# A hybrid decoder layer: the first gate/up products directly behind the last output projection, weight sums formed in place, and another layout of the PSUM banks

## The chip, the cores and the metric

The kernel runs on one core of one Trainium2 chip. The metric is the device time of one execution in microseconds; lower is better. Three runs of the kernel before gave 1325.13 to 1326.1 us, with a median of 1325.38 us.

## The reference

One decoder layer over 1024 tokens of width 1024, in float32:

```python
y = jnp.concatenate([fox_out, gla_out], axis=-1) @ w_o          # two kinds of attention
x = layer_norm(DEEPNORM_ALPHA * x + (1.0 + gate_m) * y, ln1_g, ln1_b)
u2 = x * (1.0 + scale_f) + shift_f
h = jax.nn.silu(u2 @ w_gate) * (u2 @ w_up)                      # w_gate, w_up: 1024 x 2816
y2 = h @ w_down
x = layer_norm(DEEPNORM_ALPHA * x + (1.0 + gate_f) * y2, ln2_g, ln2_b)
```

Everything ahead of `y` (the input projection, forgetting attention, gated linear attention) is the same in both kernels.

## The kernel before

**Split numbers.** Each float32 operand of a matmul is split into a high part (`hi`, rounded to the type that TensorE takes at full rate) and the rest (`lo`). `split` (L86 to L88) is one cast on ScalarE and one subtraction on VectorE. A product is the sum of three matmuls: hi x hi, hi x lo, lo x hi.

**The end of the mixer.** The output projection of the forgetting-attention half runs in units of 128 tokens x 512 columns (`mixer_units`, L830): 12 matmuls into the PSUM tile `yo`, then `yp` on VectorE (L848), a multiplication by the gate row `gm` on GpSimd (L849), the residual `r` on VectorE (L850), layer-norm statistics, and the normalisation of `r` on ScalarE (L857). `r` goes to DRAM as `z_d` (L858). There are two halves of 512 tokens with 8 units each. The `w_o` blocks for them are loaded through `load_split` into the weight pools `raw`, `hi` and `lo`, which have three buffers each; `gm` lies in a `raw` buffer until the last unit has used it.

**The feed-forward products.** Gate and up are formed together, 128 columns of each at a time ("block" `f`, 22 of them), with a Strassen-like scheme of 7 products in place of 8: the tokens are cut into two halves of 512, the input width into two halves of 512. Each product is 12 matmuls (`product`, L962): four chunks of 128 of the inner width, three matmuls each. The stationary operands are the weights `B11`, `B21` (the gate block itself), `T1` to `T4` (sums and differences of gate and up) and `B22` (half of up). The moving operands are the transposed tokens: `A11`, `A12` from the first half (`first_operands`, tiles `a1h`, `a1l`), and `A22`, `S1` to `S4` from both halves (`second_operands`, tiles `a`, `s31h`, `s31l`, `s24h`, `s24l`). `second_operands` needs the `r` of the second half, transposes it on TensorE (`u2p`, L873), evacuates it on ScalarE (L874), and forms sums and splits on VectorE and ScalarE.

**A block's products.** `load_block` fetches gate and up into two `raw` buffers. `first_weights` splits the gate block, `sum_weights` forms `t12`, `t34` in slots 4 and 5 and splits them and half of up. The products write PSUM as follows: `p12_a` (A11 x B11) and `p12_b` (A12 x B21) into the first bank of the two-bank tile `c11` (`gu` in the profile), `p6` (S2 x T2) into its second bank, `p7` (S3 x T3) and then A22 x T4 into `x_` (`gx`), `p5` (S1 x T1) and then S4 x B22 into `y_` (`gy`). ScalarE copies the sum of `p12_a` to `u` (L984) before `p12_b` adds to it; VectorE adds the second bank of `c11` to `u` (L992, `hf`). All eight banks are in use: `w0`, `w1` of two banks and `b0` to `b3`, so that two neighbouring blocks have places of their own.

**What sets the order.** The program is traced in the order of the source, which also gives the priorities; a planner then places the instructions of each engine by their readiness in its own cost estimate, gives out the buffers of the pools, and adds the waits. So TensorE's queue mixes matmuls of several products, and each engine's queue is fixed when the program runs. All loads and stores are issued by SyncE (SP) in one queue. `tc.issue_after(ins)` places what is traced under it behind `ins` in the queue of the same engine, without a wait for its end.

**Around the change.** After the last step of attention the code calls `mixer_loads(1)`, `first_operands(xa)`, the eight units of the second half, `second_operands(xb)`, the weights of blocks 0 and 1, `p12_a` and `p12_b` of both, and then the loop over the 22 blocks (L1158 to L1191). The `pt` tiles of attention lie in slots 24 and 25, the `yp` tiles of the first half in slots 4 to 7.

## Time and profile before

| | |
|---|---|
| median of 3 runs | 1325.38 us (1325.13 to 1326.1) |
| profiled execution, whole time | 1324.17 us |
| its span in the profile | 1322.5 us |
| TensorE busy | 1266.0 us (96%) |
| VectorE busy | 762.9 us (58%) |
| ScalarE busy | 487.2 us (37%) |
| granted TensorE clock, mean | 0.988 of full speed |

The busy times are those of one profiled execution, from the first to the last instruction. Matmuls overlap in the pipeline, so a busy TensorE is not one at its peak: a matmul of 512 columns shows some 390 ns, and the next one can start 0.23 us after it. Where the profile names a releaser, it is the instruction whose signal came last.

### The profile page before, as it was taken

What the parts mean: (1) busy time and instruction counts of PE and PEld (TensorE: products, weight loads), DVE (VectorE), ACT (ScalarE), POOL (GpSimd) and SP (SyncE); (2) the same over time, 40 slices, a digit from 0 to 9 for tenths busy, and PEclk for the clock granted to TensorE, in tenths of its full rate; (3) what the DMA queues carried; (4) which work ended last, traced back from release to release, by engine and by line L of the source; (5) the groups of instructions that cost most, each with busy time, mean ns of one, the idle gap of its engine ahead of it and who ended that gap; (6) DMA issues with size and microseconds to landing.
All of it is one profiled execution on the core that took longest, in us unless ns stands there. A gap on an engine that the chain in (4) does not pass through costs nothing.

```text
span 1322.5 us, 16317 instructions
## 1 busy us (share of the span) xinstructions
PE 1266.0 (96%) x6341; PEld 1017.0 (77%) x6341; DVE 762.9 (58%) x1093; ACT 487.2 (37%) x812; POOL 249.9 (19%) x244
## 2 busy tenths in 40 slices
PE   6999999999999999995999999999999999999997
PEld 4888987899876766673887777777777778778885
DVE  7665547732344536668865555565564497484346
ACT  3422255523266567465422232232232232411331
POOL 3400023320133435432000000000000087010004
PEclk9999999999999999996999999999999999999999
DMA  9865611101013207522432222222223384643431
GB/s 297 255 226 176 206 49 32 33 16 58 9 41 98 68 24 223 189 81 95 117 122 80 80 89 72 80 72 88 80 64 96 98 300 159 203 163 126 130 126 64
DMA packets 120414, 151.60 MB, mean 115 GB/s; under 512 B 6432, under 2 KB 83338, under 8 KB 120336
## 3 DMA queue, kind: packets, MB, share of 16 engines
q1 hardware_dynamic: 120336, 150.55, 35.5%
q8 instruction: 50, 0.82, 0.3%
q14 instruction: 28, 0.23, 0.1%
HBM read 122.07 MB, written 24.13 MB: 111 GB/s over the span
## 4 chain that ended last, share of the span: by engine, by line
PE 67%; issue 12%; DMA 7%; DVE 7%; ACT 3%; POOL 2%; SPq 1%; POOLq 0%; DVEq 0%; ACTq 0%
PE gu L967 11%; PE gy L967 6%; PE gx L967 6%; PE dn L1063 5%; PE dn L1064 5%; PE dn L1065 5%; PE pv L756 4%; DMA wc<-in_w_c_dram 4%; PE tr L746 3%; PE acc L330 2%; PE acc L331 2%; PE acc L332 2%; PE acc L100 2%; PE acc L101 2%; PE acc L99 2%
## 5 line engine op out<-in xcount | busy, mean ns | idle before, releaser
L87 ACT CAST hi<-raw 128x1024 fp32r<-128x1024 f32 (+1 forms) x86 | 90.0, 1049 | 289.0 <-PE gy L967 151.7
L88 DVE TENSOR_TENSOR lo<-raw,hi 128x1024 fp32r<-128x1024 f32 (+1 forms) x86 | 122.3, 1424 | 107.6 <-ACT hi L87 107.4
L1036 POOL TENSOR_TENSOR r<-r,l1g 128x1024 f32<-128x1024 f32 x8 | 26.6, 3361 | 453.8 <-DMA l1g<-in_ln_g_dram 453.8
L330 PE MATMUL acc<-hi,uh 128*128 128x264 f32 (+1 forms) x384 | 108.1, 282 | 2.1 <-ACT gr L410 1.3
L332 PE MATMUL acc<-hi,ul 128*128 128x264 f32 (+1 forms) x384 | 108.2, 282 | 0.0
L331 PE MATMUL acc<-lo,uh 128*128 128x264 f32 (+1 forms) x384 | 108.2, 282 | 0.0
L1064 PE MATMUL dn<-lo,hh 128*128 128x512 f32 x256 | 100.5, 392 | 0.0
L1065 PE MATMUL dn<-hi,hl 128*128 128x512 f32 x256 | 100.2, 392 | 0.0
L1063 PE MATMUL dn<-hi,hh 128*128 128x512 f32 x256 | 93.8, 393 | 1.4 <-ACT hi L87 1.4
L992 DVE TENSOR_TENSOR hf<-gu,hf 128x512 f32<-128x512 f32 x22 | 15.2, 691 | 133.3 <-issue 124.0
L721 DVE CUSTOM_DVE_ANT_0 pr<-sc,smask 128x128 f32<-128x128 f32 (+7 forms) x64 | 47.9, 755 | 55.3 <-PE sc L717 31.8
L967 PE MATMUL gu<-a1h,hi 128*128 128x512 f32 x168 | 69.6, 414 | 9.7 <-DVE hf L992 7.1
L87 ACT CAST hi<-t 128x1024 fp32r<-128x1024 f32 x44 | 46.1, 1050 | 85.6 <-PE gu L967 43.8
L330 PEld LDWEIGHTS acc<-hi,uh 128*128 128x128 f32 x384 | 72.2, 188 | 3.2 <-ACT gr L410 1.5
L331 PEld LDWEIGHTS acc<-lo,uh 128*128 128x128 f32 x384 | 72.2, 188 | 0.7 <-issue 0.3
L332 PEld LDWEIGHTS acc<-hi,ul 128*128 128x128 f32 x384 | 72.1, 188 | 0.3 <-issue 0.2
L88 DVE TENSOR_TENSOR lo<-t,hi 128x1024 fp32r<-128x1024 f32 x44 | 53.8, 1225 | 30.2 <-ACT hi L87 29.8
L967 PE MATMUL gu<-a1h,lo 128*128 128x512 f32 x168 | 67.7, 403 | 2.9 <-DVE lo L88 2.9
L967 PE MATMUL gu<-a1l,hi 128*128 128x512 f32 x168 | 67.4, 401 | 0.0
L731 POOL TENSOR_SCALAR pr<-pr,sm 128x128 f32<-128x128 f32 (+7 forms) x64 | 52.0, 816 | 57.5 <-DVE sm L728 57.1
L756 PE MATMUL pv<-pt,fv 128*64 128x256 f32 x320 | 61.5, 396 | 0.5 <-DVE ofl L88 0.5
L751 ACT COPY pt<-tr 128x512 f32<-128x512 f32 x80 | 46.1, 582 | 41.0 <-PE tr L746 39.2
(298 smaller groups left out, 3183.0 us busy)
## 6 DMA issues: line engine op xcount, KB each, us to landing
raw<-in_w_down_dram SPq DMA_DIRECT2D x44, 512.0 KB, 4.9
wc<-in_w_c_dram SPq DMA_DIRECT2D x32, 512.0 KB, 4.3
raw<-in_w_gate_dram SPq DMA_DIRECT2D x22, 512.0 KB, 3.9
raw<-in_w_up_dram SPq DMA_DIRECT2D x22, 512.0 KB, 4.0
h_d<-hf SPq DMA_DIRECT2D x22, 512.0 KB, 4.1
hr<-h_d SPq DMA_DIRECT2D x22, 512.0 KB, 3.8
wc<-in_w_c_dram SPq DMA_DIRECT2D x32, 256.0 KB, 6.6
raw<-in_w_in_dram SPq DMA_DIRECT2D x15, 512.0 KB, 3.9
```

Of the source, the lines that this page charges most:

```text
L87: nc.scalar.copy(dst_hi, src)
L88: nc.vector.tensor_tensor(dst_lo, src, dst_hi.bitcast(F32), op=ALU.subtract)
L330: nc.tensor.matmul(ps, uh[k][:, ts], wh[:, k % 4, :], start=k == 0, stop=False)
L331: nc.tensor.matmul(ps, uh[k][:, ts], wl[:, k % 4, :], start=False, stop=False)
L332: nc.tensor.matmul(ps, ul[k][:, ts], wh[:, k % 4, :], start=False, stop=k == NK - 1)
L721: nc.vector.tensor_tensor_reduce(t[:, 0:nk], sc[:, 0:nk], smask[:, S - nk : S], op0=ALU.add, op1=ALU.min, scale=-1.0, scalar=3e38, accum_o ...
L731: nc.gpsimd.tensor_scalar(t[:, 0:nk], t[:, 0:nk], sm[:, 2:3], 1.0, op0=ALU.mult, op1=ALU.mult)
L756: nc.tensor.matmul(pv[64 * par : 64 * par + 64, 0:256], fv_t(kb)[:, 64 * h : 64 * h + 64], pt[:, par, a * 256 : (a + 1) * 256], start=kb == 0,
L967: nc.tensor.matmul(ps, x, y, start=start and j == 0 and i == 0, stop=j == NJ - 1 and i == 2, skip_group_check=not start,)
L1063: nc.tensor.matmul(ps, hh, wh, start=i == 0 and a == 0, stop=False)
L1064: nc.tensor.matmul(ps, hh, wl, start=False, stop=False)
L1065: nc.tensor.matmul(ps, hl, wh, start=False, stop=i == NF // 2 - 1 and a == 1)
```

## The change

The last `yo` matmul is remembered in `last["yo"]`. The gate blocks 0, 1 and 2 are loaded and split early: blocks 0 and 1 ahead of the second half's units in program order, into slots 24/25 and 4/5, block 2 behind them into the weight pools. `p1` and `p2` of blocks 0 and 1 and `p1` of block 2 are traced under `after("yo")`. The loop loads the gate blocks 0 to 2 a second time for their sums. `sum_weights` forms its sums in the places of the raw gate and up blocks; up lies in slot 4 or 5 (for block 0 in a `raw` buffer). The order of the products within a block becomes `p1`, `p2`, T3, T1, T4, T2, B22. Two neighbouring blocks share one two-bank tile for `c11`, T2 has a bank of its own (`gz`, `b2` or `b3` in turn), and `x_`, `y_` are always `b0`, `b1`. ScalarE copies `x_` to `h` where VectorE added it. The transposes of `second_operands` go round four banks.

```diff
-                nc.tensor.matmul(ps, ofl[k][:, ts], wh[:, k % 2, :], start=False, stop=k == 3)
+                last["yo"] = nc.tensor.matmul(ps, ofl[k][:, ts], wh[:, k % 2, :], start=False, stop=k == 3).ins
...
-                u2_rows(rt, j + NJ * a, xs[j][:, a, :], f"b{a}")
+                u2_rows(rt, j + NJ * a, xs[j][:, a, :], ("b0", "b1", "b2", "b3")[2 * (j % 2) + a])
...
-    def load_block(f):
-        fs = slice(f * P, (f + 1) * P)
+    def load_gate(f):
         g = wtile("raw", (NK, P), F32)
-        nc.sync.dma_start(g, w_gate[:, fs].rearrange("(k p) n -> p k n", p=P))
-        u = wtile("raw", (NK, P), F32)
-        nc.sync.dma_start(u, w_up[:, fs].rearrange("(k p) n -> p k n", p=P))
-        return g, u
+        nc.sync.dma_start(g, w_gate[:, f * P : (f + 1) * P].rearrange("(k p) n -> p k n", p=P))
+        return g
+
+    def load_up(f):
+        u = wtile("raw", (NK, P), F32) if f == 0 else slot((4, 5)[f % 2], (NK, P), name="u")
+        nc.sync.dma_start(u, w_up[:, f * P : (f + 1) * P].rearrange("(k p) n -> p k n", p=P))
+        return u
...
     def sum_weights(f, g, u, w):
-        t12 = slot(4, (2, NJ, P), name="t12")
-        t34 = slot(5, (2, NJ, P), name="t34")
-        nc.vector.tensor_tensor(t12[:, 0], u[:, 0:NJ], g[:, 0:NJ], op=ALU.subtract)
-        nc.vector.tensor_tensor(t12[:, 1], u[:, NJ:NK], t12[:, 0], op=ALU.subtract)
-        nc.vector.tensor_tensor(t34[:, 0], u[:, NJ:NK], u[:, 0:NJ], op=ALU.subtract)
-        nc.vector.tensor_tensor(t34[:, 1], g[:, NJ:NK], t12[:, 1], op=ALU.subtract)
...
         b = slot((24, 25)[f % 2], (2, NJ, P), dt=F32R, name="b22")
         split(b[:, 0], b[:, 1], u[:, NJ:NK])
         w["B22"] = (b[:, 0], b[:, 1])
+        nc.vector.tensor_tensor(g[:, 0:NJ], u[:, 0:NJ], g[:, 0:NJ], op=ALU.subtract)
+        nc.vector.tensor_tensor(u[:, 0:NJ], u[:, NJ:NK], u[:, 0:NJ], op=ALU.subtract)
+        nc.vector.tensor_tensor(u[:, NJ:NK], u[:, NJ:NK], g[:, 0:NJ], op=ALU.subtract)
+        nc.vector.tensor_tensor(g[:, NJ:NK], g[:, NJ:NK], u[:, NJ:NK], op=ALU.subtract)
+        for raw, n0, n1 in ((u, "T3", "T2"), (g, "T1", "T4")):
+            h, l = wtile("hi", (NK, P), F32R), wtile("lo", (NK, P), F32R)
+            split(h, l, raw)
+            w[n0], w[n1] = (h[:, 0:NJ], l[:, 0:NJ]), (h[:, NJ:NK], l[:, NJ:NK])
...
+        if par == 0:
+            c11s[0] = wide(f"w{f // 2 % 2}", "gu")
+        c11 = c11s[0][:, par * 512 : (par + 1) * 512]
...
+        def p1():
+            product(c11, w["B11"], opnd["A11"], True)
+
+        def p2():
             h = st_["h"] = slot(6 + par, (2, 512), name="hf")
...
+            nc.scalar.copy(h[:, 0, :], c11)
+            product(c11, w["B21"], opnd["A12"], False)
+
+        def p754():
+            h = st_["h"]
+            x_ = st_["x"] = bank("b0", "gx")
             product(x_, w["T3"], opnd["S3"], True)
+            nc.scalar.copy(h[:, 1, :], x_)
+            y_ = st_["y"] = bank("b1", "gy")
             product(y_, w["T1"], opnd["S1"], True)
+            nc.vector.tensor_tensor(h[:, 1, :], y_, h[:, 1, :], op=ALU.add)
+            product(x_, w["T4"], opnd["A22"], False)
+
+        def p63():
+            x_, y_, h = st_["x"], st_["y"], st_["h"]
+            z_ = bank(("b2", "b3")[par], "gz")
+            product(z_, w["T2"], opnd["S2"], True)
+            u = h[:, 0, :]
+            nc.vector.tensor_tensor(u, z_, u, op=ALU.add)
             g = slot(HG[par], (2, 512), name="sg")
             nc.vector.tensor_tensor(g[:, 1, :], x_, u, op=ALU.add)
+            nc.vector.tensor_tensor(h[:, 1, :], h[:, 1, :], u, op=ALU.add)
+            nc.scalar.activation(g[:, 0, :], c11, AF.Silu)
+            nc.scalar.activation(g[:, 1, :], g[:, 1, :], AF.Silu)
             product(y_, w["B22"], opnd["S4"], False)
+            nc.vector.tensor_tensor(u, y_, u, op=ALU.add)
             nc.vector.tensor_tensor(h, g, h, op=ALU.mult)
             nc.sync.dma_start(h_d[f // 2][f % 2, :, :], h.rearrange("p a n -> p (a n)"))
...
     first_operands(xa)
+    ws = [{}, {}, {}]
+    first_weights(load_gate(0), ws[0], (24, 25))
+    first_weights(load_gate(1), ws[1], (4, 5))
     for f in mixer_units(1, xb, yb):
         f(3)
+    first_weights(load_gate(2), ws[2])
     second_operands(xb)
...
+    gs = [group_parts(f, ws[f]) for f in range(3)]
+    with after("yo"):
+        gs[0][0]()
+        gs[1][0]()
+        gs[0][1]()
+        gs[1][1]()
+        gs[2][0]()
     for f in range(NF):
-        if f < 2:
-            p12_a, p12_b, p6, p7, p5, mid, p43 = gs[f]
-            p6()
+        if f < 3:
+            p1, p2, p754, p63 = gs[f]
+            w = ws[f]
+            g = load_gate(f)
         else:
             w = {}
-            raws = load_block(f)
-            first_weights(raws[0], w)
-            sum_weights(f, *raws, w)
-            p12_a, p12_b, p6, p7, p5, mid, p43 = group_parts(f, w)
-            p12_a()
-            p6()
-            p12_b()
-        p7()
-        p5()
-        mid()
-        p43()
+            g = load_gate(f)
+            first_weights(g, w)
+            p1, p2, p754, p63 = group_parts(f, w)
+            p1()
+        sum_weights(f, g, load_up(f), w)
+        if f >= 2:
+            p2()
+        p754()
+        p63()
```

## Rows read from the trace of the kernel before

**Rows 1.** The page: engine totals, two costliest groups, one kind of load.

```profile
PE 1266.0 (96%) x6341; PEld 1017.0 (77%) x6341; DVE 762.9 (58%) x1093; ACT 487.2 (37%) x812; POOL 249.9 (19%) x244
...
L87 ACT CAST hi<-raw 128x1024 fp32r<-128x1024 f32 (+1 forms) x86 | 90.0, 1049 | 289.0 <-PE gy L967 151.7
...
L992 DVE TENSOR_TENSOR hf<-gu,hf 128x512 f32<-128x512 f32 x22 | 15.2, 691 | 133.3 <-issue 124.0
...
raw<-in_w_gate_dram SPq DMA_DIRECT2D x22, 512.0 KB, 3.9
```

**Rows 2.** Windows: length, busy us (instructions) PE PEld DVE ACT POOL, clock, DMA share, GB/s.

```profile
602.10:621.40 19.30, 8.97 (x34) 5.63 (x33) 13.50 (x31) 14.98 (x19) 4.75 (x6) 0.56 0.51 163
621.40:643.00 21.60, 18.69 (x65) 14.29 (x66) 21.50 (x27) 11.31 (x13) 0.00 (x0) 0.76 0.28 78
...
697.20:1040.00 342.80, 336.10 (x1431) 267.66 (x1430) 193.43 (x240) 93.97 (x120) 0.00 (x0) 1.00 0.25 80
...
613.20:643.00 29.80, 23.55 (x84) 17.43 (x84) 29.60 (x38) 19.41 (x24) 0.00 (x0) 0.69 0.34 92
```

**Rows 3.** Timeline of TensorE, 578 to 622 us: start, duration, instruction.

```profile
578.60 1.08 PE L756 MATMUL pv<-pt,fv 128*64 128x256 f32 x6
579.61 1.09 PE L873 MATMUL u2p<-ident,r 128*128 128x128 f32 x8
...
601.73 0.40 PE L847 MATMUL yo<-hi,ofl 128*128 128x512 f32 x1
...
621.38 0.80 PE L967 MATMUL gu<-a1h,hi 128*128 128x512 f32 x1 [2.62 <-ACT hi L87]
```

**Rows 4.** Timeline of VectorE, 569 to 635 us.

```profile
569.40 2.05 DVE L88 TENSOR_TENSOR lo<-raw,hi 128x1024 fp32r<-128x1024 f32 x1 [0.27 <-ACT hi L87]
...
590.84 1.22 DVE L88 TENSOR_TENSOR lo<-raw,hi 128x1024 fp32r<-128x1024 f32 x1
...
596.17 1.21 DVE L88 TENSOR_TENSOR a1l<-af,a1h 128x1024 fp32r<-128x1024 f32 x1
...
613.16 0.69 DVE L88 TENSOR_TENSOR a<-x,a 128x512 fp32r<-128x512 f32 x1 [4.25 <-ACT a L87]
...
632.99 1.22 DVE L88 TENSOR_TENSOR lo<-t,hi 128x1024 fp32r<-128x1024 f32 x1
634.13 0.69 DVE L919 TENSOR_TENSOR af<-af 128x512 f32<-128x512 f32 x1
```

**Rows 5.** Timeline of TensorE, 696 to 1060 us.

```profile
696.70 0.40 PE L967 MATMUL gu<-s24h,lo 128*128 128x512 f32 x1
...
697.17 0.40 PE L967 MATMUL gy<-s31h,lo 128*128 128x512 f32 x1
697.94 0.50 PE L967 MATMUL gu<-a1h,hi 128*128 128x512 f32 x1 [0.37 <-DVE hf L992]
...
1059.93 0.50 PE L967 MATMUL gu<-a1h,hi 128*128 128x512 f32 x1 [0.37 <-DVE hf L992]
```

**Rows 6.** Waits from 643 to 1070 us: us in total, times, longest.

```profile
PE gu L967 <- DVE hf L992: 7.1, 19, 0.4
```

**Rows 7.** Timeline of the SP queue, 567 to 611 us.

```profile
567.45 0.37 SPq L92 DMA_DIRECT2D raw<-in_w_o_dram  x1
573.43 37.38 SPq L858 DMA_DIRECT2D z_d<-r  x7
610.87 0.45 SPq L930 DMA_DIRECT2D raw<-in_w_gate_dram  x1
```

**Rows 8.** Timeline of GpSimd at 591 us.

```profile
591.06 2.15 POOL L849 TENSOR_TENSOR yp<-yp,raw 128x512 f32<-128x512 f32 x1 [3.74 <-issue]
```

**Rows 9.** Instructions of line 849, 560 to 612 us: ns min/median/max, starts.

```profile
L849 POOL TENSOR_TENSOR yp<-yp,raw x11: 1267/1290/2212, 558.9 to 604.9; 128x512 f32<-128x512 f32 x11
```

**Rows 10.** Tile `gu`: ScalarE's copy, and TensorE's idle time until it.

```profile
L984 ACT COPY hf<-gu x22: 586/587/589, 630.2 to 1051.3; 128x512 f32<-128x512 f32 x22
...
ACT hf L984: 0.5, 1
```

More of the change, by code (lines that the diff above doesn't have):

```diff
@@ L902, in second_operands @@
             for a in range(2):
-                u2_rows(rt, j + NJ * a, xs[j][:, a, :], f"b{a}")
-        dst = []
+                u2_rows(rt, j + NJ * a, xs[j][:, a, :], ("b0", "b1", "b2", "b3")[2 * (j % 2) + a])
         for j in range(NJ):
@@ L976, in group_parts @@
         par = f % 2
+        if par == 0:
+            c11s[0] = wide(f"w{f // 2 % 2}", "gu")
+        c11 = c11s[0][:, par * 512 : (par + 1) * 512]
         st_ = {}
-        def p12_a():
-            c11 = st_["c11"] = wide(f"w{par}", "gu")
+        def p1():
+            product(c11, w["B11"], opnd["A11"], True)
+        def p2():
             h = st_["h"] = slot(6 + par, (2, 512), name="hf")
-            u = st_["u"] = h[:, 0, :]
-            product(c11[:, 0:512], w["B11"], opnd["A11"], True)
-            nc.scalar.copy(u, c11[:, 0:512])
@@ L986, in p12_b @@
-        def p12_b():
-            product(st_["c11"][:, 0:512], w["B21"], opnd["A12"], False)
-        def p6():
-            u, c = st_["u"], st_["c11"]
-            product(c[:, 512:1024], w["T2"], opnd["S2"], True)
-            nc.vector.tensor_tensor(u, c[:, 512:1024], u, op=ALU.add)
-        def p7():
-            x_ = st_["x"] = bank(f"b{2 * par}", "gx")
+            nc.scalar.copy(h[:, 0, :], c11)
[3 more added lines that the diff above has]
+            x_ = st_["x"] = bank("b0", "gx")
@@ L996, in p7 @@
             product(x_, w["T3"], opnd["S3"], True)
-        def p5():
-            y_ = st_["y"] = bank(f"b{2 * par + 1}", "gy")
+            nc.scalar.copy(h[:, 1, :], x_)
+            y_ = st_["y"] = bank("b1", "gy")
             product(y_, w["T1"], opnd["S1"], True)
-        def mid():
-            h = st_["h"]
-            nc.vector.tensor_tensor(h[:, 1, :], st_["x"], st_["u"], op=ALU.add)
-            nc.vector.tensor_tensor(h[:, 1, :], st_["y"], h[:, 1, :], op=ALU.add)
-        def p43():
-            x_, y_, h, u = st_["x"], st_["y"], st_["h"], st_["u"]
+            nc.vector.tensor_tensor(h[:, 1, :], y_, h[:, 1, :], op=ALU.add)
@@ L1009, in p43 @@
+            product(x_, w["T4"], opnd["A22"], False)
[5 more added lines that the diff above has]
+            nc.vector.tensor_tensor(u, z_, u, op=ALU.add)
             g = slot(HG[par], (2, 512), name="sg")
-            product(x_, w["T4"], opnd["A22"], False)
             nc.vector.tensor_tensor(g[:, 1, :], x_, u, op=ALU.add)
+            nc.vector.tensor_tensor(h[:, 1, :], h[:, 1, :], u, op=ALU.add)
+            nc.scalar.activation(g[:, 0, :], c11, AF.Silu)
+            nc.scalar.activation(g[:, 1, :], g[:, 1, :], AF.Silu)
@@ L1012, in p43 @@
             product(y_, w["B22"], opnd["S4"], False)
-            nc.vector.tensor_tensor(h[:, 0, :], y_, u, op=ALU.add)
-            nc.scalar.activation(g[:, 0, :], st_["c11"][:, 0:512], AF.Silu)
-            nc.scalar.activation(g[:, 1, :], g[:, 1, :], AF.Silu)
+            nc.vector.tensor_tensor(u, y_, u, op=ALU.add)
             nc.vector.tensor_tensor(h, g, h, op=ALU.mult)
             nc.sync.dma_start(h_d[f // 2][f % 2, :, :], h.rearrange("p a n -> p (a n)"))
-        return p12_a, p12_b, p6, p7, p5, mid, p43
+        return p1, p2, p754, p63
@@ L1021, in hymba_layer_kernel @@
+    c11s = [None]
     HG = (14, 15)
@@ L1159, in hymba_layer_kernel @@
     first_operands(xa)
+    ws = [{}, {}, {}]
+    first_weights(load_gate(0), ws[0], (24, 25))
+    first_weights(load_gate(1), ws[1], (4, 5))
     for f in mixer_units(1, xb, yb):
         f(3)
+    first_weights(load_gate(2), ws[2])
     second_operands(xb)
-    ws = [{}, {}]
-    raws = load_block(0)
-    first_weights(raws[0], ws[0])
-    sum_weights(0, *raws, ws[0])
-    raws = load_block(1)
-    first_weights(raws[0], ws[1], (4, 5))
-    gs = [group_parts(f, ws[f]) for f in range(2)]
-    for g in gs:
-        g[0]()
-    for g in gs:
-        g[1]()
-    sum_weights(1, *raws, ws[1])
+    gs = [group_parts(f, ws[f]) for f in range(3)]
[5 more added lines that the diff above has]
+        gs[2][0]()
     for f in range(NF):
-        if f < 2:
-            p12_a, p12_b, p6, p7, p5, mid, p43 = gs[f]
-            p6()
+        if f < 3:
+            p1, p2, p754, p63 = gs[f]
+            w = ws[f]
+            g = load_gate(f)
         else:
             w = {}
-            raws = load_block(f)
-            first_weights(raws[0], w)
-            sum_weights(f, *raws, w)
-            p12_a, p12_b, p6, p7, p5, mid, p43 = group_parts(f, w)
-            p12_a()
-            p6()
-            p12_b()
-        p7()
-        p5()
-        mid()
-        p43()
+            g = load_gate(f)
[7 more added lines that the diff above has]
+        p63()
     l1g = bcast(6, ln1_g, "l1g")
```

6 lines of the change are left out of this document (removed).

## The prediction

> **What bounds the kernel now.** I began with the engine totals of the page: TensorE is busy for 96% of the span and no other engine above 77%, VectorE 58% [rows 1]. So a gain has to come from places where TensorE runs no matmul, or runs at the lower clock. The busy time by stage shows where to look [rows 2]. From 602.1 to 643.0 us, while the second half of the mixer ends and the feed-forward operands are built, TensorE is granted 0.56 and 0.76 of full speed. From 697.2 on the clock is full, and 336.1 of 342.8 us are busy.
>
> The first place in order of time [rows 3]: the last output projection matmul starts at 601.73 us, then come only the 32 transposes of `second_operands`, and the first gate/up matmul starts at 621.38 us. The waits are behind VectorE: it sits idle for 4.25 us before 613.16 [rows 4], and from 613.2 to 643 it is busy 29.6 of 29.8 us with 38 instructions [rows 2]. So VectorE ends this stage, not TensorE. By 643.0 us TensorE has done 65 of the 1848 gate/up matmuls (the 65 instructions of the window 621.4 to 643).
>
> The second place is a rhythm [rows 5]: from 697.94 us on, the first matmul of a `p12_b` stands still until `hf` L992 has read the other bank of the same `gu` tile. Elsewhere matmuls start 0.233 us apart, this one 0.77 us after its forerunner, so 0.54 us is lost, once per block of 20.11 us (697.94 to 1059.93 is 18 periods; 20.11 less 0.77, over 83, is the 0.233). The waits view counts 19 of them [rows 6]: 10.2 us.
>
> **Which time to sum against.** The profiled execution took 1324.17 us, 1.67 more than its span; the median of the runs is 1.21 above it. I sum against 1324.17 and add 1.2 at the end.
>
> **Part 1, first products behind the output projection.** Five products (`p1` and `p2` of blocks 0 and 1, `p1` of block 2) are 60 matmuls; at 0.233 us they take 14.0 us. Their operands `A11`/`A12` are complete at 597.4 us (the last `a1l` starts at 596.17 and takes 1.21 [rows 4]), so they can run from 602 on while VectorE and ScalarE build the rest. With the transposes (8 take 1.09 us at full clock [rows 3], 32 some 4.4) TensorE has work until about 620, and I count its clock as full there.
>
> What follows is still VectorE's. Of its 38 instructions, 28 are the second operands and 7 the sums of block 0. The three left, two gate splits and block 1's `b22`, are moved out or behind. A `lo` of 128x1024 costs 1.14 us from start to start (632.99 to 634.13 [rows 4]), a 512 one 0.69 [rows 1] less the same overlap of 0.08, so 0.6; together 2.9 us. The second operands and block 0's sums then end at about 640.1. By then TensorE can have done the 60, `p2` of block 2, and block 0's `T3`, `T1`, `T4` and most of `T2`, and ends `S4` by about 643.5: 132 matmuls. `T3` of block 1 cannot start yet: its sums come next on VectorE, 0.6 for `b22`, four subtractions of 0.6, a `lo` of 1.14, among three evacuations of block 0 of 0.69, some 6.2 us, so at about 646. Before, 65 + (646 − 643)/0.233 = 78 matmuls were done at 646. The lead is 54 matmuls, 12.6 us.
>
> The early splits have a price. Three gate blocks (loads of 512 KB, casts of 1.05 us [rows 1], `lo` of 1.22) now stand in or ahead of the mixer's second half. The `raw` buffers are three, and `gm` holds one to the mixer's end. Block 0's split goes to slots 24 and 25, the `pt` slots of attention, so its `raw` may be held until attention's last `pv`, at about 579.7 [rows 3]; the second half's `w_o` loads, of which the last went out at 567.45 [rows 7], would then share one buffer. The second half's projections have 34 us (568 to 602) for 96 matmuls of 0.233, 22.4 us, so there is some room. Bounds for a later end of the projection: nothing, if those loads find buffers as before, and 8 us, if the last of them goes out some 12 us later, at 579.7, and 4 us of the room swallow part. I take 2, nearer to nothing, since the room is 11.6 us.
>
> VectorE and GpSimd also hold each other up: a `lo` of 1.22 us took 2.05 at 569.40, and a `yp` that usually takes 1.29 [rows 9] took 2.15 at 591.06, beside the `lo` of 590.84 [rows 4, 8]. Three splits that each meet a `yp` cost 3 × 0.86 = 2.6 us on the chain `yp`, `r`, `mv`; that lies inside the 0 to 8. The Trainium skill ("SBUF — State Buffer", section "Who interferes with whom") speaks here against the change: a VectorE instruction with two SBUF inputs and a GpSimd one that reads SBUF block each other, and the later one waits for the whole of the first. By that rule every such meeting costs, and 2.6 us would stand in place of my 2; the two rows agree with it.
>
> The start is worth 12.6 − 2 = 10.6 us; bounds 4 (projection 8 us late) and 16 (VectorE's gap of 4.25 us takes up some 3 us of block 0's sums).
>
> The three gate blocks are loaded twice: 3 × 512 KB, landing in 3.9 us each [rows 1], where the DMA engines have a share of 0.28 [rows 2]. I count nothing; if a second load is late, block 1's sums are late by up to 3.9 us, inside the bounds.
>
> **Part 2, banks and evacuation.** `T2` goes to a bank of its own (`gz`), so `p2` no longer shares a tile with what L992 reads. `p2` still waits for ScalarE's copy of `p1`'s sum, and `T4` for a new copy of `x_` of the same kind. That copy, L984, takes 0.587 us and in 22 times held a matmul of `gu` up for 0.5 us once [rows 10], because other products stood between. Now `T3` can stand between `p1` and `p2`, and `T1` (12 matmuls, 2.8 us) stands between `T3` and `T4`. `x_` and `y_` are single now; `x_` is read last after `T2`, and `S4`, `p1`, `p2` (8.4 us) come before the next `T3`. Bounds for the wait per block: 0 and 0.54 (no change); I take 0 by the row of L984. That gives 10.2 us.
>
> ScalarE gains a copy of 0.59 us per block; it is busy 94.0 of 342.8 us there [rows 2]. VectorE keeps six evacuations per block. Both cost nothing, hidden under 19.6 us of matmuls (84 × 0.233).
>
> The transposes rotate over four banks in place of two, which takes away at most the few waits behind ScalarE among them; they lie in VectorE's stage, so nothing.
>
> **Part 3, sums in place.** The same four subtractions and three splits. They free a `hi`/`lo` pair after `p2`, `T4` and `T2`; the split of the next block's `u` then ends about 2.3 us after `T4` (1.05 + 1.22), some 9 us before its `T3`. Nothing; if this cover goes, a block waits by what is missing.
>
> **Sum.** 1324.17 − 10.6 − 10.2 = 1303.4, plus 1.2: 1304.6 us; the end of the phase and `ffn_down` move forward unchanged.
>
> **Rivals.**
> - *Both work* (above): 1304.6, own range 1298 to 1312. Chance 0.50.
> - *The rhythm stays.* `c11` of two neighbouring blocks now shares one two-bank tile, so an odd block's `p1` or `p2` may wait for a reader of the other bank, as `p12_b` does in [rows 5]. Against it: those readers (copy, Silu) can run 10 us earlier. Only the start is left: 1324.2 − 10.6 + 1.2 = 1314.8. Chance 0.20. The Trainium skill ("PSUM — Partial Sum Buffer", section "PSUM bank collisions raise a hardware error") says that accesses to different banks run clean. By it the chip asks for no such wait, and this rival would be the program's own doing; the 19 waits between two banks are there all the same.
> - *The weights come late*, and the change does not do what it says. SP's seven `z_d` stores took from 573.43 to 610.8, and the first gate load went out behind them at 610.87 [rows 7]. If the early loads fall behind them again, or hold up `w_o` by the full 8 us, some 2 us of the start remain: 1324.2 − 2 − 10.2 + 1.2 = 1313.2. Chance 0.17.
> - *Slower: ScalarE's copies in the product chain.* If nothing stands between `p1` and `p2`, and casts stand ahead of the copy of `x_`, each copy costs TensorE about 0.9 us: in [rows 5] the last matmul that L992 waits for starts at 696.70 and `p12_b` 1.24 us later, 0.69 of it L992; with 0.59 in its place it is 1.14, less the 0.233 that a matmul takes anyhow. That is 1.8 per block in place of 0.54: 19 × 1.26 = 24 us lost against 10.6 gained, 1324.2 + 13.4 + 1.2 = 1339. It decides from 1.1 us of waits per block, (10.6 + 10.2)/19. Against it: L984's 0.5 us. Chance 0.09.
> - The rest, 0.04: gains and losses that cancel.
>
> About 0.2% (2.6 us) is what measurements of this kernel can tell from no change. Faster 0.87, same 0.04, slower 0.09. The range takes in the first three cases: from 1324.2 − 16 − 10.2 + 1.2, about 1299, with 3 us below it for a VectorE stage that ends still earlier, to 1324.2 − 4 + 1.2, about 1322. So 1296 to 1322.
>
> **What would show it.** Right: `gu` matmuls 0.233 us apart directly behind the last `yo`, a granted clock near 1 from 602 to 643, 132 matmuls done at about 646, block periods near 19.6 us with no wait on VectorE. Wrong: a last `yo` after 606; TensorE waiting for block 1's `lo` for over 6 us; a wait per block on a copy or on VectorE; periods above 20.1. The likeliest step to fail is the end of VectorE's stage near 640, since it hangs on how the planner mixes the sums of blocks 0 and 1 into the second operands.

## The result and the profile after

The changed kernel takes 1315.8 us (median of 4 runs, 1315.33 to 1316.62) against 1325.41 us for the kernel before on the same chip (4 runs, 1325.13 to 1326.1): ratio 0.9927, 95% interval 0.991 to 0.9945. The gain is 9.6 us where 20.8 were forecast. The time lies inside the range, the sign is right, the size is off by half.

The totals of the page, after:

```profile
span 1314.2 us, 16370 instructions
PE 1259.9 (96%) x6341; PEld 1018.3 (77%) x6341; DVE 756.2 (58%) x1093; ACT 497.1 (38%) x834; POOL 244.6 (19%) x244
```

The same windows as in [rows 2], after:

```profile
core 0: us, PE busy (x) PEld busy (x) DVE busy (x) ACT busy (x) POOL busy (x), PEclk, DMA share, GB/s
602.00:621.40 19.40, 19.40 (x102) 16.14 (x100) 11.41 (x25) 9.23 (x12) 7.38 (x8) 1.00 0.46 151
621.40:643.00 21.60, 7.73 (x23) 5.09 (x23) 21.53 (x31) 15.40 (x20) 0.00 (x0) 0.68 0.24 63
643.00:697.20 54.20, 54.20 (x230) 44.07 (x229) 36.38 (x46) 16.40 (x22) 0.00 (x0) 0.97 0.44 134
697.20:1040.00 342.80, 342.80 (x1482) 279.19 (x1481) 199.86 (x251) 105.78 (x142) 0.00 (x0) 1.00 0.25 79
```

Two readings. From 697.2 on TensorE is busy for the whole window: the 19 waits are gone. From 602 to 621 it is now busy all the time and its clock is full, but from 621 to 643 it does only 23 instructions and the clock falls to 0.68. The work was moved forward, and the hole moved behind it.

TensorE's timeline shows the hole, and two new waits where `ffn_down` begins (a selection of its rows, in order of time):

```profile
606.56 0.39 PE L847 MATMUL yo<-hi,ofl 128*128 128x512 f32 x1
606.79 0.40 PE L965 MATMUL gu<-a1h,b 128*128 128x512 f32 x1
617.30 0.60 PE L873 MATMUL u2p<-ident,r 128*128 128x128 f32 x4
619.60 1.91 PE L873 MATMUL u2p<-ident,r 128*128 128x128 f32 x16
624.11 0.39 PE L965 MATMUL gu<-a1h,b 128*128 128x512 f32 x1
637.60 0.79 PE L965 MATMUL gx<-s31h,hi 128*128 128x512 f32 x1 [13.10 <-ACT hi L87]
645.47 0.63 PE L965 MATMUL gx<-s31l,hi 128*128 128x512 f32 x1
...
1063.96 0.50 PE L1059 MATMUL dn<-hi,hh 128*128 128x512 f32 x1 [0.94 <-DVE sg L1005]
1066.94 0.51 PE L1059 MATMUL dn<-hi,hh 128*128 128x512 f32 x1 [1.11 <-DVE hf L1010]
```

The last `yo` starts at 606.56, not at 601.73 [rows 3]. The 60 early matmuls follow 0.23 us apart, with the transposes among them, the last one at 624.11. Then TensorE waits 13.10 us for the `hi` of block 0's weight sums. Its first 17 matmuls behind the hole come mostly 0.43 us apart until 645.9; from 630 to 646 us the granted clock is 0.50 of full speed (1.2 GHz).

VectorE's and ScalarE's timelines show what the sums were waiting for:

```profile
620.93 0.69 DVE L88 TENSOR_TENSOR a<-x,a 128x512 fp32r<-128x512 f32 x1 [6.24 <-ACT a L87]
635.43 0.68 DVE L953 TENSOR_TENSOR raw<-raw,raw 128x512 f32<-128x512 f32 x1
646.53 2.35 DVE L88 TENSOR_TENSOR s24l<-af,s24h 128x1024 fp32r<-128x1024 f32 x2
```

```profile
614.73 1.24 ACT L857 ACTIVATE r<-r,mv 128x1024 f32<-128x1024 f32 x1 [0.21 <-DVE mv L854]
617.61 2.78 ACT L874 ACTIVATE x<-u2p,mcol 128x512 f32<-128x512 f32 x4 [1.64 <-PE u2p L873]
620.28 0.63 ACT L87 CAST a<-x 128x512 fp32r<-128x512 f32 x1
636.50 1.04 ACT L87 CAST hi<-raw 128x1024 fp32r<-128x1024 f32 x1
```

VectorE begins the second operands at 620.93, 7.8 us later than before (613.16 [rows 4]), and is through with them at 648.9, where the end of the second operands and block 0's sums was forecast at 640.1. The cast at 636.50 that TensorE waits for stands right behind VectorE's subtraction L953 at 635.43.

Counted along TensorE's timelines, in us (the n-th gate/up matmul, the 100th of `ffn_down`, and the span's end):

| | before | after | difference grows by |
|---|---|---|---|
| last `yo` | 601.73 | 606.56 | |
| 132nd | 658.28 | 658.74 | +0.5 (the start) |
| last gate/up | 1069.02 | 1058.22 | -11.3 (the blocks) |
| 100th of `ffn_down` | 1091.18 | 1081.88 | +1.5 |
| end of span | 1322.5 | 1314.2 | +1.0 |

The two spans differ by 8.3 us; the medians of the runs differ by 9.6. Part of the 0.5 lies ahead of the change. TensorE's first 3200 matmuls stand in the same order in every run of this document, but the 3200th, which opens a row of transposes, starts at another time in each profiled execution; before and after:

```profile
559.84 0.60 PE L746 MATMUL tr<-ident,pr 128*128 128x128 f32 x4
```

```profile
559.26 0.60 PE L746 MATMUL tr<-ident,pr 128*128 128x128 f32 x4
```

Counted from that matmul, the last `yo` comes 5.4 us later than before, VectorE's stage ends 6.6 us later, and the start loses 1.1 us. Where times of two runs are compared below as "counted from the 3200th matmul", this difference is taken off.

So the whole gain comes from the blocks. The start, forecast at 10.6 us, gave nothing, and `ffn_down` takes 2.5 us back.

### The profile page after: what moved, and what is told of

The parts are those of the page before. It is cut to its first block, busy times and chain, and to the rows that moved or that the text cites. A ratio compares the mean times of both kernels' runs of the same rounds, so it can differ in the third digit from the quotient of the medians.

```text
span 1314.2 us, 16370 instructions
## 1 busy us (share of the span) xinstructions
PE 1259.9 (96%) x6341; PEld 1018.3 (77%) x6341; DVE 756.2 (58%) x1093; ACT 497.1 (38%) x834; POOL 244.6 (19%) x244
## 4 chain that ended last, share of the span: by engine, by line
PE 77%; DMA 8%; DVE 7%; ACT 3%; issue 2%; POOL 1%; SPq 1%; POOLq 0%; DVEq 0%; ACTq 0%
PE gx L965 9%; PE gy L965 9%; PE gu L965 9%; DMA wc<-in_w_c_dram 5%; PE dn L1059 5%; PE dn L1061 5%; PE dn L1060 5%; PE gz L965 5%; PE pv L756 4%; PE tr L746 3%; PE acc L330 2%; PE acc L331 2%; PE acc L332 2%; PE acc L100 2%; PE acc L101 2%
## 5 line engine op out<-in xcount | busy, mean ns | idle before, releaser
L88 DVE TENSOR_TENSOR lo<-raw,hi 128x1024 fp32r<-128x1024 f32 (+1 forms) x108 | 146.3, 1356 | 258.6 <-ACT hi L87 258.5
L87 ACT CAST hi<-raw 128x1024 fp32r<-128x1024 f32 (+1 forms) x108 | 113.1, 1049 | 192.3 <-PE dn L1061 79.3
L965 PE MATMUL gu<-a1h,hi 128*128 128x512 f32 x160 | 63.6, 397 | 0.0
L965 PE MATMUL gu<-a1l,hi 128*128 128x512 f32 x160 | 63.5, 397 | 0.0
L965 PE MATMUL gu<-a1h,lo 128*128 128x512 f32 x160 | 63.3, 396 | 0.0
L1059 PEld LDWEIGHTS dn<-hi,hh 128*128 128x128 f32 x256 | 48.2, 189 | 16.6 <-ACT hi L87 2.8
L100 PE MATMUL acc<-ul,hi 128*128 128x512 f32 x144 | 58.0, 403 | 0.0
L101 PE MATMUL acc<-uh,lo 128*128 128x512 f32 x144 | 57.9, 402 | 0.0
```

Of the source, the lines that this page charges most:

```text
L87: nc.scalar.copy(dst_hi, src)
L88: nc.vector.tensor_tensor(dst_lo, src, dst_hi.bitcast(F32), op=ALU.subtract)
L100: nc.tensor.matmul(ps, lh, rl, start=False, stop=False)
L101: nc.tensor.matmul(ps, ll, rh, start=False, stop=stop)
L965: nc.tensor.matmul(ps, x, y, start=start and j == 0 and i == 0, stop=j == NJ - 1 and i == 2, skip_group_check=not start,)
L1059: nc.tensor.matmul(ps, hh, wh, start=i == 0 and a == 0, stop=False)
```

## The experiments

Each was timed against the kernel before on its own chip; ratios compare across groups, since that kernel's median lay between 1324.95 and 1326.34. "After" is the changed kernel, 0.9927 (0.991 to 0.9945). Where two intervals overlap, the times alone do not tell the kernels apart, and what is said of them rests on the traces. The code cuts leave out lines where `...` stands.

**What made the 19 waits: order or tile.** In the kernel before, `p6` and `p12_b` of the loop were exchanged, nothing else:

```diff
             p12_a()
-            p6()
             p12_b()
+            p6()
```

> The kernel before with two calls swapped: in the loop p12_b is traced ahead of p6, so T2's product and the VectorE read L992 of the second bank come after both products of the first bank; T2 stays in the second bank of the same tile. Theory as predicted (the shared two-bank tile causes the wait): products into that tile go on waiting for readers of the other bank, period 20.11 us, 1325 us. Rival (the order causes it: p12_b is traced behind L992, so it has to wait): the 19 waits of 0.54 us are gone, period near 19.57 us, 1315 us.

1314.64 us, ratio 0.991 (0.9895 to 0.9925). The window from 697.2 on shows TensorE full:

```profile
697.20:1040.00 342.80, 342.80 (x1482) 279.07 (x1482) 200.00 (x246) 96.45 (x124) 0.00 (x0) 1.00 0.26 82
```

From the other side, the order was kept and T2's product got a bank of its own:

```diff
-            u, c = st_["u"], st_["c11"]
-            product(c[:, 512:1024], w["T2"], opnd["S2"], True)
-            nc.vector.tensor_tensor(u, c[:, 512:1024], u, op=ALU.add)
+            u = st_["u"]
+            z_ = bank(("b2", "b3")[par], "gz")
+            product(z_, w["T2"], opnd["S2"], True)
+            nc.vector.tensor_tensor(u, z_, u, op=ALU.add)
...
-            x_ = st_["x"] = bank(f"b{2 * par}", "gx")
+            x_ = st_["x"] = bank("b0", "gx")
...
-            y_ = st_["y"] = bank(f"b{2 * par + 1}", "gy")
+            y_ = st_["y"] = bank("b1", "gy")
```

> The kernel before, but T2's product goes to a bank of its own (b2 or b3), with one x and one y bank in place of two; the order p12_a, p6, p12_b is kept, and p12_b now shares no tile with what the VectorE addition of T2 reads. Theory A, that of the prediction (the wait comes from the shared two-bank tile): the 19 waits of 0.54 us go although the order stays, about 1315.0 us. Theory B (the order alone, with the bank without weight): the waits stay, 1325. Swapping the order alone gave 1314.6; if this gives the same, tile and order are both needed for the wait, and removing either is enough. If single x and y banks add waits, they show as waits on the evacuations of x and y.

1313.7 us, ratio 0.9907 (0.9894 to 0.992); no wait of TensorE from 697 to 1060. The wait needed both: a tile shared with the reader, and the matmul behind that reader in program order. Taking either away is enough, and either alone gives what the whole change gives, within the intervals. In the second of these kernels the order is that of the kernel before, and T2's sum lies in another bank than `p12_b`'s, as it did before; only the shared tile is gone, and the wait with it. So the wait came from the program, which treated the tile as a whole, and not from the banks. That agrees with the Trainium skill ("PSUM — Partial Sum Buffer", section "PSUM bank collisions raise a hardware error"): accesses to different banks run clean.

**What the early products are worth.** The changed kernel without them and without what they need (no early gate blocks, no second loads, no `after("yo")`; the blocks 0 to 2 are made in the loop like all others):

> The changed kernel without its early start: no early gate blocks, no products behind the last output projection, no second loads; blocks 0 to 2 run as all others; banks, order of products and sums in place as changed. Theory now (the early start brought nothing in the end, all of the gain is the lost wait per block): 1315.8 us within 3, the last yo back at about 602 us. Rival (the prediction's term: the early start is worth about 10 us, and something else took its gain): about 1326 us.

1322.14 us, ratio 0.9976 (0.9965 to 0.9986). The early products, with the price of their loads, bring 6.3 us to this layout. But the layout's plain start is 6.2 us worse than the old one, counted from the 3200th matmul (the 132nd gate/up matmul starts at 665.4, before at 658.3): the last `yo` starts at 602.73, and TensorE waits twice for weights. Which part of the layout (the order of the products, the sums in place, the banks) costs this was not tested.

```profile
620.99 0.79 PE L965 MATMUL gu<-a1h,hi 128*128 128x512 f32 x1 [4.84 <-ACT hi L87]
638.34 0.79 PE L965 MATMUL gx<-s31h,hi 128*128 128x512 f32 x1 [5.92 <-ACT hi L87]
```

**Who holds the output projection up.** The raw gate blocks 0 and 1 in slots 6 and 7, out of the `raw` pool:

```diff
...
-    first_weights(load_gate(0), ws[0], (24, 25))
-    first_weights(load_gate(1), ws[1], (4, 5))
+    first_weights(load_gate(0, 6), ws[0], (24, 25))
+    first_weights(load_gate(1, 7), ws[1], (4, 5))
```

> The changed kernel with the first loads of gate blocks 0 and 1 in slots 6 and 7 in place of two raw buffers. Theory (these two loads hold the raw buffers that the w_o loads of the second half need, which makes the projection end 5 us later): the w_o loads go out at about 555 and 567 us again, the last yo matmul starts at 602 to 603 us in place of 606.6, and the time falls by 3 to 5 us, to about 1312 us. Rival (the projection is late because the moved splits collide with VectorE's and GpSimd's chain): last yo still near 606, 1315.8 us.

1312.83 us, ratio 0.9899 (0.9887 to 0.9912). The last `yo` starts 2.6 us earlier by the span's clock, and 3.9 us earlier counted from the 3200th matmul: of the 5.4 us by which the change had delayed it, 3.9 were these two buffers. The hole behind it keeps its size:

```profile
603.96 0.39 PE L847 MATMUL yo<-hi,ofl 128*128 128x512 f32 x1
634.98 0.80 PE L965 MATMUL gx<-s31h,hi 128*128 128x512 f32 x1 [13.09 <-ACT hi L87]
```

In the changed kernel the last `w_o` load goes out at 581.51, before at 567.45 [rows 7], here at 568.12:

```profile
566.86 8.35 SPq L92 DMA_DIRECT2D raw<-in_w_o_dram  x2
576.50 0.37 SPq L92 DMA_DIRECT2D raw<-in_w_o_dram  x1
581.51 0.38 SPq L92 DMA_DIRECT2D raw<-in_w_o_dram  x1
```

Only two early gate blocks and 48 early matmuls (block 2's load, split and `p1` back in the loop):

> The changed kernel with only two early gate blocks and four early products (48 matmuls); the load, split and first product of block 2 go back into the loop. Theory A (the early gate blocks hold up the mixer's second half): the last output projection ends earlier than 606.56, by 1 to 2 us, and with it VectorE's stage, with its lo (1.2 us) less; the time falls to 1313 to 1315. Theory B (12 products fewer behind the projection weigh as much, 2.8 us): 1316 to 1318.

1316.87 us, ratio 0.9938 (0.9925 to 0.9952): the last `yo` starts at 604.99 and VectorE's stage ends 2.5 us earlier (1.2 and 2.1 counted from the 3200th matmul), but the 132nd gate/up matmul comes at 658.6, after at 658.7. What the third block costs, its 12 matmuls give back.

**Who sets the hole behind the early products.** Five edits of the changed kernel, all of which failed to help. The sums of block 0 traced ahead of S2 and S4:

```diff
...
+    def second_sums(xs):
...
+        if f == 0:
+            second_sums(xs2)
```

> The changed kernel with second_operands cut in two: the sums of block 0 are traced ahead of the operands S2 and S4 (which only T2 and B22 need). Theory (block 0's sums stand too far back in VectorE's queue, so TensorE has nothing to do for 13.1 us and falls to the lower clock): T3 of block 0 starts at 628 to 632 us in place of 637.6, the wait is under 8 us, 1311 to 1313 us. Rival (VectorE ends the stage at 649 us whatever the order, and TensorE waits there instead, for S2 and S4): first wait shorter, a second one appears, 1315 to 1316 us.

1317.77 us, ratio 0.9938 (0.9926 to 0.995): the wait stays at 13.12 us. The queues are mixed by readiness, and in the two traces every engine has the same instructions in the same order as in the changed kernel. So this run says nothing of another order. It is a second measurement of the same program: 0.9938 and 0.9927, 1317.77 and 1315.8 us, show by how much two such medians can differ.

Transposes over two banks again:

```diff
-                u2_rows(rt, j + NJ * a, xs[j][:, a, :], ("b0", "b1", "b2", "b3")[2 * (j % 2) + a])
+                u2_rows(rt, j + NJ * a, xs[j][:, a, :], f"b{a}")
```

> The changed kernel, but the transposes of the second operands rotate over two banks again in place of four. In the changed kernel ScalarE clears four x tiles in a row (617.61, 2.78 us) before the first cast of a that VectorE waits for, and VectorE starts its stage at 620.93, 4.96 us after the last r is done; in the kernel before it was some 1.6 us. Theory A (the four banks put two more x tiles, 1.4 us, ahead of that cast): VectorE starts near 619.5, and the time falls by about 1.4 us to 1314.4. Theory B (only the later projection and the products ahead of the transposes delay VectorE): no change, 1315.8, or a little slower if transposes now wait for banks.

1318.54 us, ratio 0.9945 (0.9932 to 0.9958), no gain: two `x` fewer stood ahead of the cast, but the transposes now waited for banks and for the products queued between them; TensorE's wait grew to 15.39 us.

The products behind the transposes in TensorE's queue, first two of them, then three (the cut shows three):

```diff
...
         gs[0][0]()
         gs[1][0]()
+    with after("u2p"):
         gs[0][1]()
         gs[1][1]()
```

> The changed kernel, but of the five early products only the first three stand directly behind the last output projection; the other two (24 matmuls) are issued behind the last transpose of the second operands. In the changed kernel the last r is done at 615.97, but TensorE's queue has products ahead and the last transposes start at 617.30 and 619.60. Theory A (the early products delay the transposes, and with them VectorE's stage, which ends the start): transposes at about 616, VectorE starts 1.2 us earlier, near 619.7, and the time falls by 1 to 1.5 us to about 1314.5, with no loss for the two products, since TensorE has idle time behind them. Theory B (VectorE's start hangs on ScalarE's casts and not on the transposes): no change, 1315.8.

> The changed kernel, but only the two p1 of blocks 0 and 1 (24 matmuls, 5.6 us) stand directly behind the last output projection; the other three products are issued behind all 32 transposes of the second operands. Moving only the last two had left 12 products between the third and the fourth r, so the transposes of the last r still started 1.5 us late. Now nothing stands ahead of them. Theory A (products ahead of the transposes in TensorE's queue are what delays VectorE's stage, start 620.93 and 4.96 us after the last r): VectorE starts 3.3 us after the last r, the stage ends some 1.7 us earlier and the time falls to about 1314. Theory B (ScalarE's queue of x, copies and casts sets it): less than 0.7 us, 1315 to 1316.

1318.7 us, ratio 0.994 (0.9926 to 0.9953), and 1319.07 us, ratio 0.995 (0.9937 to 0.9963). Counted from the 3200th matmul, the 132nd gate/up matmul comes as after with two moved, and 1.5 us later with three. With three moved, the transposes are no longer late (the first `x` comes 0.42 us after the last `r`), but now five `x` stand ahead of the cast:

```profile
617.07 1.24 ACT L857 ACTIVATE r<-r,mv 128x1024 f32<-128x1024 f32 x1 [0.21 <-DVE mv L854]
618.73 3.46 ACT L874 ACTIVATE x<-u2p,mcol 128x512 f32<-128x512 f32 x5 [0.42 <-PE u2p L873]
622.06 0.64 ACT L87 CAST a<-x 128x512 fp32r<-128x512 f32 x1
```

So ScalarE's order was fixed by itself, two `x`, then the cast:

```diff
-        nc.scalar.activation(dst, ps, AF.Identity, bias=mcol[:, 4, k : k + 1], scale=mcol[:, 5, k : k + 1])
+        with after(key):
+            nc.scalar.activation(dst, ps, AF.Identity, bias=mcol[:, 4, k : k + 1], scale=mcol[:, 5, k : k + 1])
...
+                u2_rows(rt, j + NJ * a, xs[j][:, a, :], ("b0", "b1", "b2", "b3")[2 * (j % 2) + a], "a22")
...
+            last["a22"] = nc.scalar.copy(t[:, 0, :], xs[j][:, 1, :]).ins
```

> The changed kernel with one order fixed on ScalarE: the two x tiles of an operand are made only after the cast of a of the operand before, so the first cast stands behind two x tiles in place of four, over the same four banks. With the products moved behind the transposes VectorE started 0.5 us sooner after the last r, and ScalarE had put five x tiles (3.46 us) ahead of that cast. Theory A (ScalarE's order of x tiles and casts delays VectorE): VectorE starts 1.3 us earlier, near 619.6, and the time falls by 1 to 1.3 us, to about 1314.6. Theory B (VectorE's stage then runs into later waits for x or casts and ends as late): 1315.8.

1318.18 us, ratio 0.9945 (0.9932 to 0.9959). VectorE starts 1.2 us sooner after the last `yo` (607.35 here) and ends 0.7 us sooner after it (at 649.0), but the cast of block 0's sums came later, and TensorE waits 15.11 us. Counted from the 3200th matmul the 132nd gate/up matmul is 0.1 us later than after, although VectorE's stage ends sooner:

```profile
640.49 0.80 PE L964 MATMUL gx<-s31h,hi 128*128 128x512 f32 x1 [15.11 <-ACT hi L87]
```

**VectorE's work on GpSimd.** The weight sums of blocks 0 and 1:

```diff
+        eng = nc.gpsimd if f < 2 else nc.vector
...
-        nc.vector.tensor_tensor(g[:, 0:NJ], u[:, 0:NJ], g[:, 0:NJ], op=ALU.subtract)
...
+        eng.tensor_tensor(g[:, 0:NJ], u[:, 0:NJ], g[:, 0:NJ], op=ALU.subtract)
...
```

> The changed kernel, but the four subtractions of the weight sums of blocks 0 and 1 run on GpSimd in place of VectorE. VectorE is busy without a gap from 620.9 to 648.9; eight subtractions of 0.6 us are 4.8 us of it. Theory A (VectorE's amount of work sets the end of the stage): the stage ends some 4 us earlier, TensorE's wait of 13.1 us shortens, time near 1312 to 1313. Theory B (VectorE and GpSimd hold each other up, as in the rows where a lo of 1.22 took 2.05 us): GpSimd's subtractions take 1.3 us or more each, eight are over 10 us, VectorE's rows beside them grow by as much, and the time stays or rises, 1316 to 1320.

1324.47 us, ratio 0.9991 (0.998 to 1.0003): by the ratios some 8.5 us worse than after. GpSimd's and VectorE's rows beside each other:

```profile
631.04 6.26 POOL L954 TENSOR_TENSOR raw<-raw,raw 128x512 f32<-128x512 f32 x1 [5.44 <-DVE b L88]
648.28 1.59 POOL L954 TENSOR_TENSOR u<-u,raw 128x512 f32<-128x512 f32 x1
```

```profile
644.74 2.31 DVE L88 TENSOR_TENSOR s31l<-x,s31h 128x1024 fp32r<-128x1024 f32 x1
648.67 2.28 DVE L88 TENSOR_TENSOR s31l<-raw,s31h 128x1024 fp32r<-128x1024 f32 x1
```

One subtraction took 6.26 us on GpSimd, where one of the same size took 1.59, and a `lo` 2.3 us on VectorE. This agrees with the Trainium skill ("SBUF — State Buffer", section "Who interferes with whom"): a VectorE instruction that takes both operands from SBUF and a GpSimd one that reads SBUF lock each other out.

**Where `ffn_down` gives gains back.** With the slots as above, the last two pairs of accumulators were exchanged, so that `b2` and `b3` are written before `b0` and `b1`; then three early products moved behind the transposes as well:

```diff
-                    acc.append(bank(f"b{2 * (q - 2) + d}", "dn"))
+                    acc.append(bank(f"b{2 * (3 - q) + d}", "dn"))
```

> The changed kernel with the raw gate blocks 0 and 1 in slots 6 and 7 (that alone: 1312.8, ratio 0.9899), and with the last two pairs of accumulators of ffn_down exchanged, so that b2 and b3 are written before b0 and b1. In the changed kernel ffn_down waits 0.94 and 1.11 us for the readers of b0 and b1 at 1063.96 and 1066.94, which stand on VectorE behind a lo of 3.42 us. Theory A (only the order of the banks makes these waits): both go, 2 us less, about 1311, ratio near 0.9885. Theory B (VectorE is late there whatever is written first): other waits of the same length come in their place, 1312.8.

> The three edits together: raw gate blocks in slots 6 and 7, three of the early products behind the transposes, accumulators of ffn_down exchanged. If the gains add: 1315.8 - 3.0 - 1.7 - 2 = about 1309. If the start gives back what one edit saves (VectorE's stage is set by its own 28 us of work and its start): 1311, as without the change of the products.

1313.26 us, ratio 0.9908 (0.9894 to 0.9923), and 1312.9 us, ratio 0.9904 (0.9889 to 0.9918): no better than the slots alone. In the first the two waits are gone, which brings 2.1 us from the last gate/up to the 100th `dn` matmul, but a later wait for a down weight's cast grew to 3.3 us (1.4 before, 2.1 after, 2.5 with the slots):

```profile
PE dn L1059 <- ACT hi L87: 3.3, 1, 3.3
```

The kept down weights then got buffers of their own:

```diff
-                raw = wtile("raw", (2, 512), F32)
+                raw = cp.tile([P, 2, 512], F32, tag=("c4a", "c4b")[d], name=nm("kr"))
```

> The kernel with the raw gate blocks in slots 6 and 7 and the accumulators exchanged, and besides the six kept down-weight loads of each half of ffn_down take two buffers of their own (c4a, c4b) in place of the three raw buffers. There the two waits at the start of ffn_down are gone, 2.3 us earlier at the 100th matmul, but the end came no earlier: a wait of TensorE for the cast of a down weight at about 1140 us grew to 3.3 us (1.4 in the kernel before, 2.1 in the changed one), behind kept loads in SP's queue that wait for raw buffers. Theory A (these buffers hold the loads up and give the gain back): the wait at 1140 goes or falls below 1 us, and the time falls by 2 to 3 us, to about 1310.5. Theory B (the DMA stream itself is the bound there): the wait stays near 3 us and the time at 1313.

1312.58 us, ratio 0.9907 (0.9892 to 0.9922). That wait fell to 0.2 us, and one of 4.2 us for the last block's `hf` came in its place:

```profile
PE dn L1059 <- DVE hf L1010: 4.2, 1, 4.2
PE dn L1059 <- ACT hi L87: 0.2, 1, 0.2
```

All of it together (slots, accumulators, kept buffers, cast first, three products behind the transposes):

> All that has helped or should: raw gate blocks in slots 6 and 7, accumulators exchanged, kept down weights in buffers of their own, the first cast behind two x tiles, and three of the early products behind the transposes. If the gains add to the 1312.8 of the slots: 2 us at the start of ffn_down, 1.8 us of VectorE's earlier start, so about 1309; if VectorE's stage gives its part back, 1310.5; if the start of ffn_down does as well, 1312.8.

1311.23 us, ratio 0.9889 (0.9875 to 0.9903). The start now works: VectorE begins at 614.49, and the 132nd gate/up matmul comes at 653.0. Counted from the 3200th matmul that is 4.4 us earlier than before. The kernel with slots, accumulators and kept buffers alone is 3.2 us earlier there, so the two orders together (cast first, three products behind the transposes) bring 1.2 us; VectorE's stage ends 1.5 us sooner after the last `yo` by them. But TensorE waits 4.4 us for `hf` at the last block, where GpSimd multiplies eight rows by the layer-norm gain beside VectorE:

```profile
1044.57 25.21 POOL L1031 TENSOR_TENSOR r<-r,l1g 128x1024 f32<-128x1024 f32 x8 [434.24 <-DVE lo L88]
```

```profile
1047.98 3.43 DVE L88 TENSOR_TENSOR lo<-raw,hi 128x1024 fp32r<-128x1024 f32 x1
1054.69 3.42 DVE L88 TENSOR_TENSOR lo<-raw,hi 128x1024 fp32r<-128x1024 f32 x1
1064.14 0.68 DVE L1009 TENSOR_TENSOR hf<-gy,hf 128x512 f32<-128x512 f32 x1
```

The last experiment made GpSimd start later by exchanging two slots, with the queues of TensorE, VectorE and ScalarE unchanged:

```diff
-    l1g = bcast(6, ln1_g, "l1g")
-    l1b = bcast(7, ln1_b, "l1b")
+    l1g = bcast(7, ln1_g, "l1g")
+    l1b = bcast(6, ln1_b, "l1b")
```

> The kernel of all gains (1311.2), with the slots of ln1's gain and bias rows exchanged, so that the gain is loaded only when the last gate/up block has left slot 7. The orders of TensorE, VectorE and ScalarE stay; GpSimd's eight products with that gain, which ran from 1044.57 on beside VectorE's last block (a lo of 1.22 us took 3.42 there), start some 20 us later. Theory A (GpSimd's work beside VectorE makes the last block's sums late, and TensorE's wait of 4.4 us for hf with them): those lo take 1.2 us again, the wait goes, and the time falls by about 4 us to 1307. Theory B (the wait comes from the order of VectorE's queue alone): the wait stays above 3 us, 1311. A third way: GpSimd then meets VectorE inside ffn_down and the 4 us come back there as a wait for a cast or lo.

1309.35 us, ratio 0.9883 (0.9866 to 0.9899), the lowest of all, by less than the interval. The first three rows show VectorE before GpSimd's work begins, at 1073.40, the last one beside it:

```profile
1046.69 1.23 DVE L88 TENSOR_TENSOR lo<-raw,hi 128x1024 fp32r<-128x1024 f32 x1 [1.49 <-ACT hi L87]
1050.51 1.22 DVE L88 TENSOR_TENSOR lo<-raw,hi 128x1024 fp32r<-128x1024 f32 x1
1053.98 0.68 DVE L1009 TENSOR_TENSOR hf<-gy,hf 128x512 f32<-128x512 f32 x1
1087.37 3.42 DVE L88 TENSOR_TENSOR lo<-raw,hi 128x1024 fp32r<-128x1024 f32 x1
```

```profile
1119.92 0.79 PE L1059 MATMUL dn<-lo,hh 128*128 128x512 f32 x1 [3.55 <-DVE lo L88]
```

`hf` L1009 comes 10 us earlier and its wait is gone, so GpSimd's work had made it. Then GpSimd meets VectorE inside `ffn_down` (the `lo` at 1087.37), and 3.55 us come back as another wait: the third way. The span falls from 1309.6 to 1307.4, by 1.4 us counted from the 3200th matmul; by the ratios the two kernels can't be told apart.

## Why the prediction was right in sign and wrong in size

**The rhythm (10.2 us): right.** Its 19 waits are gone, and from the 132nd gate/up matmul to the last 11.3 us were gained. The blame on the shared tile was half of the cause: the own bank alone removes the waits, but so does the order alone. The rivals *the rhythm stays* and *copies in the chain* are refuted by the full window from 697.2 on; that the 1314.8 of *the rhythm stays* lies nearest to the measured time is luck.

**The start (10.6 us): wrong, about -1.1 counted from the 3200th matmul.** The step that failed is the one named as likeliest to fail: "The second operands and block 0's sums then end at about 640.1". VectorE's stage ended at 648.9; counted from the 3200th matmul that is 9.4 us later than forecast. Of these, 5.4 are the later projection (2 were allowed for, apart from the 640.1). 3.0 come because VectorE starts 14.4 us after the last `yo` where it was 11.4 (forecast at nothing). 1.0 comes because two instructions of block 1, of 0.6 us each, stand inside the stage, which takes 28.0 us and not 26.9.

Another 4.0 us are TensorE's: it passed the 132nd matmul 9.9 us after that end, where the prediction had 5.9 (646). The 17 matmuls behind the hole, from 637.60 to 646.30, took 8.7 us, 0.8 of it a wait; 0.23 us apart they take 4.0, so the clock cost 3.9. With the 2 taken off, 7.4 and 4.0 make 11.4 of the 11.7 us missed; the kernel before, which passed its 132nd at 658.3 where the prediction's working gives 658.6, makes the rest.

- The projection: "nothing, if those loads find buffers as before, and 8 us" held as bounds. The mechanism was named (the `raw` buffers), the value was taken too near to nothing: 3.9 of the 5.4 us are these buffers, by the slots. Of the rest, the third early block may have a part (without it the last `yo` came 1.2 us earlier), but it was not taken apart. `yp` L849 on GpSimd took 4.38 us for two beside a `lo` there, which points to the two engines' meetings, but no run shows it.
- VectorE's start: products stand between the transposes, and four `x` ahead of the first cast. Moving three products brought 0.5 us at VectorE's start, after the last `yo`, but its stage ended 1.2 us later; the cast first brought 1.2 us at the start and 0.7 at the end. Both together, beside the slots, brought the start to 12.1 us after the last `yo`, 1.5 us at the stage's end and 1.2 us at the 132nd matmul.
- The sums: TensorE's wait of 13.1 us hangs on where the planner puts them in VectorE's queue. No run moved them ahead, so what a better order would give stays open. Behind the wait TensorE stood still once more, for 0.77 us, up to the 132nd matmul: its restart at 637.60 and the clock set the start, and the end of VectorE's stage by itself did not.
- The work for the hole: by the end of VectorE's stage the prediction has the 60, `p2` of block 2, `T3`, `T1`, `T4` and most of `T2`, some 117 matmuls (132 at 643.5, less 3.4 us of them); 89 were done. 12 of the missing 28 are `p2` of block 2, which could not run there. Its `h` lies in slot 6, like block 0's (`slot(6 + par)`), and the loop calls it behind block 0's products: block 0's `h` was stored at 660.20, ScalarE's copy for `p2` came at 663.37, and its first matmul at 667.75. Some 2.8 us of work for the hole were thus out of reach; no run gave it a slot of its own.

```profile
660.20 0.34 SPq L1012 DMA_DIRECT2D h_d<-hf  x1
663.37 0.59 ACT L985 COPY hf<-gu 128x512 f32<-128x512 f32 x1
667.75 0.40 PE L965 MATMUL gu<-a1h,hi 128*128 128x512 f32 x1
```

- The layout: sums in place, order and banks were costed at nothing for the start. Without the early products the new layout passes the 132nd matmul 6.2 us later than the kernel before, so the early products paid for the layout first. Why it is later was not tested.
- The clock: "I count its clock as full" was right from 602 to 621 and wrong behind it, 0.68 up to 643.

**Costed at nothing, and not free.** "the end of the phase and `ffn_down` move forward unchanged": they gave back 2.5 us, two waits of 0.94 and 1.11 us for `b0` and `b1` and a longer wait for a down weight. The rival *the weights come late* (1313.2) described the start best: it had the mechanism and left 2 us.

## What to carry to other kernels

Work pulled ahead of a stage pays only if the stage's own end moves: follow each engine's queue to that end, with the buffers that the early work holds and the places where it stands ahead of others. Before two tiles are rearranged, try the order of two products; here two exchanged lines gave the gain of the whole change. A gain upstream has to survive the next place where another engine sets the pace, so look there for a wait that will grow.

## What the runs showed of the hardware that was not expected

- A `lo` of 1.22 us took 3.42 us beside GpSimd's multiplications of 128x1024 (3.15 us each), while VectorE additions that read PSUM, such as `hf` L1009, stayed at 0.68 us in the same stretch.
- After 13.1 us without a matmul, matmuls of 512 columns came 0.43 us apart for 8 us, from 637.6 to 645.9, and then 0.23 again. The granted clock was 0.50 (1.2 GHz) from 630 to 646 and 1.00 from 646.5 on.
